# Third group's statistics and the factors on GpSimd's queue, and the first group's products with V without zero blocks

## The chip, the cores and the metric

The kernel runs on one core of a Trainium2 chip, as one program. A core has TensorE (PE in the profile; its weight loads are listed as PEld), VectorE (DVE), ScalarE (ACT), GpSimd (POOL) and SyncE (SP), which here only issues transfers. Each engine takes its own instructions strictly in the program's order and waits for the others by semaphores. Transfers are issued from SP, ACT or POOL, and 16 DMA engines carry them. The metric is the device time of one execution in microseconds (us); lower is better. The profile adds one recorded execution with the start, length and cause of waiting of each instruction.

## The reference, cut to what matters

Two layers work on x of 1024 tokens by 1024 features, all in float32. The first layer is dilated sliding-window attention with 18 heads of 64 features in three groups of six; the second is a latent attention that the change does not touch. In group 0 a query sees the 64 keys on either side of it, in group 1 the same at a stride of 4, in group 2 at a stride of 16. The three groups are merged with weights that come from the softmax statistics.

```
DIL_GROUPS = ((128, 1), (512, 4), (2048, 16))

s = einsum('bdhnqe,bdhnke->bdhnqk', qs, kb) * (Dh ** -0.5) + bias[:, None]
s = where(valid, s, NEG_INF)          # |key - query| <= R, R = window // (2 * dil) = 64
m = s.max(-1, keepdims=True)
p = exp(s - m)
denom = p.sum(-1, keepdims=True)
o = einsum('bdhnqk,bdhnke->bdhnqe', p, vb) / denom
lse = (m + log(denom))[..., 0]

# mixer_dilated
wts = softmax(stack(lses, axis=0), axis=0)
o = concatenate([outs[g] * wts[g][..., None] for g in range(len(DIL_GROUPS))], axis=2)
y = o.reshape(B, S, WIDTH_A) * silu(gate)
return y @ w_out
```

## The kernel before, in words

**Precision.** Most products are made of two or three matmuls on a reduced float32 type (`F32R`). An operand is split into a high part, which ScalarE rounds, and a low part, which VectorE or GpSimd gets by subtraction. A projection is then high by high, high by low and low by high (`mm3`, lines 89 to 91). A product with V in groups 0 and 1 splits only the probabilities (tiles `pt0h` and `pt0l`, line 550), since V's tile holds its own high and low halves side by side. Group 2 multiplies plain float32.

**Attention of layer A.** There are nine pairs of heads, three to a group. The attention of pair p is woven with the projection of pair p+1, a block of 128 weight columns at a time; `weave` picks at each step the generator that is furthest behind, by costs that the program states (`a_cost`). A pair has eight units of two query tiles (256 queries of one head). Each unit passes through `front` (scores on PE, line 487 and 488; bias and minimum on DVE, line 495; exponential on ACT, line 501), `middle` (transposes on PE, line 512; high part on ACT, line 528; low part on DVE, line 529) and `back` (product with V on PE, line 550).

**Products with V in group 0.** Two query tiles of 128 see three key tiles: the first only by the first query tile, the second by both, the third only by the second. `back` multiplies each of the three by 256 columns, so a unit has six matmuls of 256 columns (three key tiles, high and low part). The columns of the query tile that does not see a key tile are blocks of zeros in `pt0h` and `pt0l`, which are set once at the start (line 609). Two units share a PSUM bank, each with its own half.

**Merging.** After pair 8, `merge_lines` transposes the statistics (minimum and sum) of the groups. Those of groups 1 and 2 are in the order of the stride and are put in token order through DRAM: per group two writes (line 671) and twelve loads of 4 KB (line 675). VectorE then computes the factors, which go to DRAM (line 701) and come back as rows spread over 64 partitions (`factors`, line 709). `y_block` multiplies a pair's output by its factors (DVE, line 717) and by the gate (POOL, line 718).

**Gate blocks.** While this goes on, PE computes the gate projection: nine blocks of 128 columns, two of them during pair 8's attention and seven (blocks 2 to 8) in `layer_a_gate`. Each block needs 512 KB of weights, which SP loads (`w_load`, line 96, tile `wraw`), ACT rounds (line 101, `wh`) and POOL completes (line 102, `wl`). A block is 48 matmuls of 512 columns (the `pj` rows).

**What sets the order.** PE and SP run in the order in which the code is written. On the other engines a scheduler orders the instructions within its dependences. SP's order around the merge is: loads of group 1's and group 2's statistics, then the writes of the factors, then the weights of gate block 4 and the blocks after it. Line numbers are those of the profile of the kernel before.

Of the kernel before, what the change touches and what calls it, by code (L numbers as in the profile page):

```python
# [15 lines left out]
F32 = mybir.dt.float32  # L16
F32R = mybir.dt.float32r
# [6 lines left out]
P = 128  # L24
# [17 lines left out]
def f32(ap):  # L42
    return ap.bitcast(F32)


def weave(*gens):

    live = [[g, 0.0, float(total)] for g, total in gens]
    while live:
        it = min(live, key=lambda e: e[1] / e[2])  # L50
        try:
            it[1] += next(it[0])
        except StopIteration:
            live.remove(it)


def steps(gen, n):
    for _ in itertools.islice(gen, n):
        yield 1.0
# [7 lines left out]
class Trunk:  # L67
# [380 lines left out]
    def a_units(self, p):  # L448
        g = p // 3
        return 4 if g < 2 else 2  # L450

    def a_attn(self, p):

        nc = self.nc
        g, d = p // 3, self.a_dst[p]
        o = self.o[p] = self.gt(F32, "o")
        stat = self.stat[g]
        n = 8
        st = {}
        stage = self.zq[g == 2]  # L460

        def staged(i):

# [43 lines left out]
        def middle(i):  # L507
            sb = st.pop(i)
            pt = self.bank("t")
            nb = 4 if g < 2 else 2  # L510
            for j in range(nb):
                nc.tensor.transpose(pt[:, j * P : j * P + P], sb[:, j * P : j * P + P], self.ident)
            if g == 2:
                h = self.KP.tile([P, 256], F32, tag="ot", bufs=3, name=self.nm("pt2"))
                nc.vector.tensor_copy(h, pt[:, 0:256])
                st[i] = (h, None)
                return
            src = pt.rearrange("p (a b c) -> p a b c", a=2, b=2)
            if g == 0:
                h, l = self.pt0[i % 2]  # L520
                vh, vl = (
                    t.rearrange("p (a m) -> p a m", m=384)[:, :, :].rearrange("p a (b c) -> p a b c", c=P)[:, :, 0:3:2, :]
                    for t in (h, l)
                )
            else:
                h, l = self.pt0[i % 2]
                vh, vl = (t[:, 0:512].rearrange("p (b a c) -> p a b c", a=2, b=2) for t in (h, l))
            nc.scalar.copy(vh, src)
            nc.vector.tensor_tensor(vl, src, f32(vh), op=ALU.subtract)
            st[i] = (h, l)  # L530

        def back(i):
            e, up = i // 4, i % 4
            h, l = st.pop(i)
            if up % 2 == 0:
                st["o"] = self.bank("o")
            po = st["o"]
            if g == 2:
                for a in range(2):
                    t = 2 * up + a  # L540
                    c0 = (up % 2) * 256 + a * P
                    nc.tensor.matmul(
                        po[:, c0 : c0 + P], d["vt"][:, t, :], h[:, a * P : a * P + P], start=True, stop=True
                    )
            else:
                out = po[:, (up % 2) * 256 : (up % 2) * 256 + 256]
                nk = 3 if g == 0 else 2
                for k in range(nk):
                    for x, part in enumerate((h, l)):
                        nc.tensor.matmul(  # L550
                            out, d["vt"][:, 2 * up + k, e, :], part[:, k * 256 : k * 256 + 256],
                            start=(k == 0 and x == 0), stop=(k == nk - 1 and x == 1),
                        )
            if up % 2 == 1:
                z = up // 2
                mine, other = slice(64 * e, 64 * e + 64), slice(64 - 64 * e, 128 - 64 * e)
                ov = o[mine, :]
                if g == 0:
                    src, dst = (lambda x: x), ov[:, z * 512 : z * 512 + 512]
                elif g == 1:  # L560
                    src = lambda x: x.rearrange("p (r j) -> p r j", r=2)
                    dst = ov.rearrange("p (j r) -> p r j", r=4)[:, 2 * z : 2 * z + 2, :]
                else:
                    src = lambda x: x.rearrange("p (i j) -> p i j", i=4)
                    dst = ov.rearrange("p (j i) -> p i j", i=8)[:, 4 * z : 4 * z + 4, :]
# [25 lines left out]
                back(i - 2)  # L591
                yield cost[2]

    a_cost = ((480.0, 440.0, 720.0), (480.0, 440.0, 480.0), (480.0, 220.0, 480.0))

    def layer_a_attention(self):
        nc = self.nc
        self.o = {}
        for g in (1, 2):
            self.bias_line(g)  # L600
            self.bias_write(g)
        self.rows_d = self.DR.tile([2, 1, 1024], F32, name="rows_d")
        nc.vector.tensor_copy(self.ones_r, self.ones.to_broadcast([P, P]))
        self.pt0 = []
        for i in range(2):
            hl = []
            for x in "hl":
                t = self.KP.tile([P, 768], F32R, name=f"pt0{x}{i}")
                nc.gpsimd.memset(f32(t), 0.0)
                hl.append(t)  # L610
            self.pt0.append(hl)
        self.zq = []
        for x, dt in (("r", F32R), ("f", F32)):
            self.zq.append([[self.KP.tile([P, 256], dt, name=f"zq{x}{e}{i}") for i in range(2)] for e in range(2)])
            for e in range(2):
                for t in self.zq[-1][e]:
                    nc.gpsimd.memset(f32(t)[64 - 64 * e : 128 - 64 * e, :], 0.0)
# [31 lines left out]
    def merge_lines(self):  # L649


        nc = self.nc
        X, Y = self.ht(F32, "X"), self.ht(F32, "Y")
        part = lambda t, i, n=1: t[0:48, i * P : (i + n) * P]
        stat_d = self.DR.tile([2, 2, 48, P], F32, name="stat_d")
        self.f_d = self.DR.tile([3, 6, 1024], F32, name="f_d")
        for g in (1, 2, 0):
            pl = self.bank("pl")
            for s in range(2):
                nc.tensor.transpose(  # L660
                    pl[0:48, s * P : s * P + P], self.stat[g][:, s].rearrange("p h t -> p (h t)"), self.ident
                )
            if g == 0:
                for s in range(2):
                    nc.scalar.copy(part(X, 3 * s), pl[0:48, s * P : s * P + P])
                continue
            t = part(Y, 2 * g, 2)
            nc.scalar.copy(t, pl[0:48, 0:256])
            n = 32 if g == 1 else 16
            for s in range(2):  # L670
                nc.sync.dma_start(stat_d[g - 1, s], t[:, s * P : s * P + P])
            for s in range(2):
                ld = stat_d[g - 1, s]
                for h in range(6):
                    nc.sync.dma_start(
                        X[8 * h : 8 * h + 8, (3 * s + g) * P : (3 * s + g + 1) * P].rearrange("p (r j) -> p r j", j=n),
                        bass.AP(ld.tensor, ld.offset + 1024 * h, [[n, 8], [8 * n, P // n], [1, n]]),
                    )
# [19 lines left out]
        V.reciprocal(part(Y, 6), part(Y, 3))  # L698
        for g in range(3):
            V.tensor_tensor(part(Y, g), part(Y, g), part(Y, 6), op=ALU.mult)  # L700
            nc.sync.dma_start(self.f_d[g].rearrange("h (b t) -> (h b) t", t=P), part(Y, g))
        self.fs = {}

    def factors(self, b):
# [842 lines left out]
```

## Time and profile before

| | before |
|---|---|
| median of 3 runs | 1391.44 us |
| the three runs | 1387.54, 1391.44, 1395.55 us |
| the profiled execution: its time, its span | 1394.88 us, 1393.1 us |
| PE busy | 1346.1 us, 97% of the span |
| DVE, ACT, POOL busy | 918.1, 812.9, 570.5 us |
| mean granted clock of PE | 0.993 |
| attention of layer A | about 65 to 480 us of the span |
| merge and gate blocks 2 to 8 | 483 to 566 us |

The tables used are the page of the profile; the list of who waited for whom by engine; the timelines of single engines, where equal neighbours are merged and a row has start, length, engine, line, operation and, in brackets, the idle time before it and what ended it; the table of stretches, which has for each stretch its length, then busy time and number of instructions of PE, PEld, DVE, ACT and POOL, the clock that PE was granted, the share of the DMA engines and GB/s; and the answers for one line or tile, which give minimum, median and maximum length in ns. A matmul's row shows its whole passage through the array, 0.28 to 0.40 us, which overlaps with the next one's; what a matmul takes of PE's time is the distance between two starts.

### The profile page before, as it was taken

Reading aid. Unit: us, or ns where it says so; the run is one execution under the profiler, and the core shown is the slowest. Engines: PE = TensorE matmul, PEld = TensorE weight load, DVE = VectorE, ACT = ScalarE, POOL = GpSimd, SP = SyncE. Lnnn points to the kernel's source line nnn. Section 1 sums busy time; section 2 is a strip of 40 time slices with the busy share of each in tenths; the row PEclk is TensorE's granted clock in tenths of the full one; section 3 lists DMA queues with packets and bytes.
Section 4 is the critical chain, followed back from the end, with each engine's and each line's share of the span. In section 5 each row is a group of like instructions: output and inputs, shape, how many; then the busy total and the mean of one; then the engine's idle time right before and its main releaser. Section 6 shows DMA issues by size and latency. Waiting matters only on the chain.

```text
span 1393.1 us, 20960 instructions
## 1 busy us (share of the span) xinstructions
PE 1346.1 (97%) x7463; PEld 1153.6 (83%) x7463; DVE 918.1 (66%) x1688; ACT 812.9 (58%) x1599; POOL 570.5 (41%) x653
## 2 busy tenths in 40 slices
PE   6999999999999989999999999999999999999897
PEld 5788888888888878888987888888889888898786
DVE  7655454554455433646744178898988889888787
ACT  3565565565444432436742188788687878888321
POOL 6342243132123135803742254634453463444653
PEclk9999999999999999999999999999999999999999
DMA  9322211022244346544144001010011100014132
GB/s 362 95 70 36 61 45 55 24 61 65 83 152 130 100 114 154 191 143 158 47 130 155 22 22 29 16 30 16 22 30 24 30 16 16 16 61 130 53 109 88
DMA packets 42808, 110.05 MB, mean 79 GB/s; under 512 B 6853, under 2 KB 13205, under 8 KB 42704
## 3 DMA queue, kind: packets, MB, share of 16 engines
q1 hardware_dynamic: 38696, 96.60, 22.6%
q0 software_dynamic: 3552, 12.06, 3.5%
q8 instruction: 59, 0.97, 0.3%
q14 instruction: 45, 0.37, 0.1%
q10 hardware_dynamic: 456, 0.05, 0.0%
HBM read 92.22 MB, written 8.61 MB: 72 GB/s over the span
## 4 chain that ended last, share of the span: by engine, by line
PE 68%; DVE 16%; ACT 6%; issue 5%; DMA 3%; SPq 1%; POOL 0%; DVEq 0%; ACTq 0%; POOLq 0%
PE pj L91 7%; PE pj L89 7%; PE pj L90 6%; PE o L1305 5%; PE t L1282 5%; DVE mb L1263 3%; PE s L91 3%; PE s L89 3%; PE s L90 3%; PE po L91 3%; PE po L89 3%; PE po L90 3%; PE pg L89 2%; PE pg L91 2%; PE pg L90 2%
## 5 line engine op out<-in xcount | busy, mean ns | idle before, releaser
L89 PE MATMUL pj<-uh,wh 128*128 128x512 f32 x528 | 216.5, 410 | 2.1 <-ACT wh L101 2.1
L91 PE MATMUL pj<-uh,wl 128*128 128x512 f32 x528 | 207.9, 394 | 1.6 <-POOL wl L102 1.6
L90 PE MATMUL pj<-ul,wh 128*128 128x512 f32 x528 | 207.7, 393 | 0.0
L1286 DVE TENSOR_TENSOR ptl<-t,pth 128x512 fp32r<-128x512 f32 x256 | 165.3, 681 | 3.0 <-ACT pth L1285 0.9
L1263 DVE TENSOR_REDUCE mb<-s 128x1 f32<-128x1024 f32 x128 | 155.7, 1217 | 7.9 <-PE s L91 6.3
L1269 ACT ACTIVATE pr<-s,mb 128x1024 f32<-128x1024 f32 x128 | 143.4, 1120 | 29.2 <-DVE mb L1263 21.1
L1285 ACT CAST pth<-t 128x512 fp32r<-128x512 f32 x256 | 138.9, 590 | 36.2 <-PE t L1282 34.1
L102 POOL TENSOR_TENSOR wl<-wraw,wh 128x1024 fp32r<-128x1024 f32 x43 | 107.5, 2506 | 106.0 <-ACT wh L101 60.9
L1282 PEld LDWEIGHTS t<-ident,pr 128*128 128x128 f32 x1024 | 119.3, 140 | 19.7 <-DVE ptl L1286 2.6
L1282 PE MATMUL t<-ident,pr 128*128 128x128 f32 x1024 | 133.2, 272 | 1.9 <-DVE ptl L1286 1.9
L1305 PE MATMUL o<-pth,vq 128*128 128x256 f32 x512 | 130.4, 293 | 0.0
L1305 PE MATMUL o<-ptl,vq 128*128 128x256 f32 x512 | 125.5, 283 | 0.8 <-DVE ptl L1286 0.8
L501 ACT ACTIVATE sb<-sb,stat 128x256 f32<-128x256 f32 (+1 forms) x144 | 67.0, 467 | 97.5 <-DVE stat L495 97.3
L91 PEld LDWEIGHTS pj<-uh,wl 128*128 128x128 f32 x528 | 99.7, 189 | 24.3 <-POOL wl L102 2.1
L89 PEld LDWEIGHTS pj<-uh,wh 128*128 128x128 f32 x528 | 100.3, 190 | 16.8 <-ACT wh L101 2.5
L1288 POOL COPY den<-mb 128x64 f32<-128x64 f32 x128 | 30.1, 237 | 202.9 <-DVE mb L1287 193.3
L90 PEld LDWEIGHTS pj<-ul,wh 128*128 128x128 f32 x528 | 100.4, 190 | 14.3
L89 PE MATMUL s<-kb,q 128*128 128x512 f32 x256 | 104.4, 408 | 0.2 <-ACT pr L1269 0.2
L91 PE MATMUL s<-kb,q 128*128 128x512 f32 x256 | 101.3, 396 | 0.0
L90 PE MATMUL s<-kb,q 128*128 128x512 f32 x256 | 100.8, 394 | 0.0
L1305 PEld LDWEIGHTS o<-ptl,vq 128*128 128x128 f32 x512 | 97.8, 191 | 1.4 <-DVE ptl L1286 1.4
L1305 PEld LDWEIGHTS o<-pth,vq 128*128 128x128 f32 x512 | 97.7, 191 | 0.2
(281 smaller groups left out, 3262.6 us busy)
## 6 DMA issues: line engine op xcount, KB each, us to landing
wraw<-wa SPq DMA_DIRECT2D x36, 512.0 KB
ada<-ada_row SPq DMA_DIRECT2D x64, 256.0 KB
wraw<-wo_a SPq DMA_DIRECT2D x18, 512.0 KB
ada<-ada_ss SPq DMA_DIRECT2D x16, 512.0 KB
kb<-kb POOLq DMA_DIRECT2D x30, 256.0 KB, 3.0
f<-f_d SPq DMA_DIRECT2D x18, 256.0 KB
xc<-xt SPq DMA_DIRECT2D x8, 512.0 KB
xr<-x SPq DMA_DIRECT2D x8, 512.0 KB
```

The costliest lines, as they stand in the source:

```text
L89: mm(out, wh, xh, start=start, stop=False)
L90: mm(out, wh, xl, start=False, stop=False)
L91: mm(out, wl, xh, start=False, stop=stop)
L102: (lo_engine or self.nc.gpsimd).tensor_tensor(l[:, :width], raw[:, :width], f32(h[:, :width]), op=ALU.subtract)
L501: nc.scalar.activation(sb[:, a * w : a * w + w], sb[:, a * w : a * w + w], AF.Exp, bias=stat[:, 0, hh, t : t + 1], scale=-1.0, accum_out=s ...
L1263: nc.vector.tensor_reduce(m[:, 0:1], s, axis=AX.X, op=ALU.max, negate=True)
L1269: nc.scalar.activation(pr, s, AF.Exp, bias=m[:, 0:1], accum_out=m[:, 1:2])
L1282: nc.tensor.transpose(pt[:, c * P : c * P + P], pr[:, kt * P : kt * P + P], self.ident)
L1285: nc.scalar.copy(h, src)
L1286: nc.vector.tensor_tensor(l, src, f32(h), op=ALU.subtract)
L1288: nc.gpsimd.tensor_copy(st["den"][:, 64 * a : 64 * a + 64], m[:, 2:3].to_broadcast([P, 64]))
L1305: nc.tensor.matmul(po[:, 0:256], v, pts[j][x][:, c * 256 : c * 256 + 256], start=n == 0, stop=n == 15)
```

## The change

It has two parts.

**The queue.** Group 2's statistics (two writes, twelve loads) and all three factor writes are issued from POOL's queue; group 1's statistics stay on SP.

**Products with V in group 0.** The tiles `pt0h` and `pt0l` become 1024 wide and hold two units (four query tiles) without zeros. Four query tiles see five key tiles. An even unit multiplies key tile 1 (256 columns) and 0 (128 columns), an odd unit key tiles 3 and 2 (256 columns each) and 4 (128 columns), each for the high and the low part. So a pair of units has ten matmuls, six of 256 and four of 128 columns, in place of twelve of 256. All of them add into one bank; only the first sets the start flag. The stated cost of `back` in group 0 goes from 720 to 580.

To make room, the tiles with padded queries (`zq`) exist once: they are made for group 0 as `F32R` and again for group 2 as `F32`, where they are cleared again. The clearing of `pt0` falls away.

```
@@ def zero_padded, a_attn @@
+    def zero_padded(self, dt):
+        z = [
+            [self.KP.tile([P, 256], dt, tag=f"zq{e}{i}", bufs=1, name=self.nm("zq" + "fr"[dt == F32R])) for i in range(2)]
+            for e in range(2)
+        ]
+        for e in range(2):
+            for t in z[e]:
+                self.nc.gpsimd.memset(f32(t)[64 - 64 * e : 128 - 64 * e, :], 0.0)
+        return z
...
-        stage = self.zq[g == 2]
+        if p % 3 == 0 and g != 1:
+            self.zq = self.zero_padded(F32R if g == 0 else F32)
+        stage = self.zq
@@ middle @@
-            src = pt.rearrange("p (a b c) -> p a b c", a=2, b=2)
+            half = self.pt0[i // 2 % 2]
+            h, l = (t[:, i % 2 * 512 : i % 2 * 512 + 512] for t in half)
             if g == 0:
-                h, l = self.pt0[i % 2]
-                vh, vl = (
-                    t.rearrange("p (a m) -> p a m", m=384)[:, :, :].rearrange("p a (b c) -> p a b c", c=P)[:, :, 0:3:2, :]
-                    for t in (h, l)
-                )
+                vh, vl, src = h, l, pt
+                st[i] = half
             else:
-                h, l = self.pt0[i % 2]
-                vh, vl = (t[:, 0:512].rearrange("p (b a c) -> p a b c", a=2, b=2) for t in (h, l))
+                vh, vl = (t.rearrange("p (b a c) -> p a b c", a=2, b=2) for t in (h, l))
+                src = pt.rearrange("p (a b c) -> p a b c", a=2, b=2)
+                st[i] = (h, l)
             nc.scalar.copy(vh, src)
             nc.vector.tensor_tensor(vl, src, f32(vh), op=ALU.subtract)
-            st[i] = (h, l)
@@ back @@
+            elif g == 0:
+                z = up - up % 2
+                for k in ((1, 0), (3, 2, 4))[up % 2]:
+                    c0, c1 = max(256 * k - P, 0), min(256 * k + P, 1024)
+                    q0 = max(P * (k - 1), 0)
+                    for x, part in enumerate((h, l)):
+                        nc.tensor.matmul(
+                            po[:, q0 : q0 + (c1 - c0)], d["vt"][:, 2 * z + k, e, :], part[:, c0:c1],
+                            start=(k == 1 and x == 0), stop=(k == 4 and x == 1), skip_group_check=True,
+                        )
             else:
                 out = po[:, (up % 2) * 256 : (up % 2) * 256 + 256]
-                nk = 3 if g == 0 else 2
-                for k in range(nk):
+                for k in range(2):
...
-    a_cost = ((480.0, 440.0, 720.0), (480.0, 440.0, 480.0), (480.0, 220.0, 480.0))
+    a_cost = ((480.0, 440.0, 580.0), (480.0, 440.0, 480.0), (480.0, 220.0, 480.0))
@@ layer_a_attention @@
         for i in range(2):
-            hl = []
-            for x in "hl":
-                t = self.KP.tile([P, 768], F32R, name=f"pt0{x}{i}")
-                nc.gpsimd.memset(f32(t), 0.0)
-                hl.append(t)
-            self.pt0.append(hl)
-        self.zq = []
...
+            self.pt0.append([self.KP.tile([P, 1024], F32R, name=f"pt0{x}{i}") for x in "hl"])
@@ merge_lines @@
-            n = 32 if g == 1 else 16
+            n, queue = (32, nc.sync) if g == 1 else (16, nc.gpsimd)
             for s in range(2):
-                nc.sync.dma_start(stat_d[g - 1, s], t[:, s * P : s * P + P])
+                queue.dma_start(stat_d[g - 1, s], t[:, s * P : s * P + P])
...
-                    nc.sync.dma_start(
+                    queue.dma_start(
...
-            nc.sync.dma_start(self.f_d[g].rearrange("h (b t) -> (h b) t", t=P), part(Y, g))
+            nc.gpsimd.dma_start(self.f_d[g].rearrange("h (b t) -> (h b) t", t=P), part(Y, g))
```

**SP's queue at the merge.** `stat_d` and `X` are the statistics on their way through DRAM, `f_d` the factors, `wraw` the weights of gate blocks 3, 4, 5 and 6 in this order. First before, then changed:

```order
L96 DMA wraw_625_4150<-wa 128x1024
L671 DMA stat_d_4193<-Y_629_4192 48x128 x2
L675 DMA X_628_4191<-stat_d_4193 8x4x32 x12
L671 DMA stat_d_4193<-Y_629_4192 48x128 x2
L675 DMA X_628_4191<-stat_d_4193 8x8x16 x12
L701 DMA f_d_4194<-Y_629_4192 48x128 x3
L96 DMA wraw_638_4300<-wa 128x1024
L96 DMA wraw_644_4359<-wa 128x1024
L709 DMA f_645_4374<-f_d_4194 64x1024 x2
L709 DMA f_646_4377<-f_d_4194 64x1024 x2
L96 DMA wraw_652_4424<-wa 128x1024
```

```order
L96 DMA wraw_633_4122<-wa 128x1024
L682 DMA stat_d_4165<-Y_637_4164 48x128 x2
L686 DMA X_636_4163<-stat_d_4165 8x4x32 x12
L96 DMA wraw_646_4272<-wa 128x1024
L96 DMA wraw_652_4331<-wa 128x1024
L720 DMA f_653_4346<-f_d_4166 64x1024 x2
L720 DMA f_654_4349<-f_d_4166 64x1024 x2
L96 DMA wraw_660_4396<-wa 128x1024
```

The weights of gate blocks 4 and 5 (`wraw_638` and `wraw_644`, now `wraw_646` and `wraw_652`) stand behind seventeen transfers fewer.

**POOL's queue at the merge.** `wl` are the low parts of the weights of gate blocks 3, 4, 5 and, in the last row, 6; `o` are the outputs multiplied by the gate. First before, then changed:

```order
L102 TENSOR_TENSOR wl_636_4283<-wraw_625_4150,wh_635_4282 128x1024
L102 TENSOR_TENSOR wl_642_4342<-wraw_638_4300,wh_641_4341 128x1024
L102 TENSOR_TENSOR wl_650_4407<-wraw_644_4359,wh_649_4406 128x1024
L718 TENSOR_TENSOR o_99_616<-o_99_616,graw_576_3877 128x1024
L718 TENSOR_TENSOR o_151_1021<-o_151_1021,graw_607_4049 128x1024
L102 TENSOR_TENSOR wl_657_4471<-wraw_652_4424,wh_656_4470 128x1024
```

```order
L102 TENSOR_TENSOR wl_644_4255<-wraw_633_4122,wh_643_4254 128x1024
L682 DMA stat_d_4165<-Y_637_4164 48x128 x2
L686 DMA X_636_4163<-stat_d_4165 8x8x16 x12
L102 TENSOR_TENSOR wl_650_4314<-wraw_646_4272,wh_649_4313 128x1024
L712 DMA f_d_4166<-Y_637_4164 48x128 x3
L102 TENSOR_TENSOR wl_658_4379<-wraw_652_4331,wh_657_4378 128x1024
L729 TENSOR_TENSOR o_99_596<-o_99_596,graw_584_3849 128x1024
L729 TENSOR_TENSOR o_155_1001<-o_155_1001,graw_615_4021 128x1024
L102 TENSOR_TENSOR wl_665_4443<-wraw_660_4396,wh_664_4442 128x1024
```

Fourteen transfers now stand ahead of gate block 4's low part, and three more ahead of block 5's.

**PE at the first odd unit of group 0.** `t` are transposes, `o` the product with V. First before, then changed:

```order
L512 MATMUL t_770<-ident,sb_705 128x128 x4
L550 MATMUL o_740<-pt0h_563,vt_663 128x256
L550 MATMUL o_740<-pt0l_565,vt_663 128x256
L550 MATMUL o_740<-pt0h_563,vt_663 128x256
L550 MATMUL o_740<-pt0l_565,vt_663 128x256
L550 MATMUL o_740<-pt0h_563,vt_663 128x256
L550 MATMUL o_740<-pt0l_565,vt_663 128x256
```

```order
L564 MATMUL o_728<-pt0h_559,vt_651 128x256
L564 MATMUL o_728<-pt0l_560,vt_651 128x256
L564 MATMUL o_728<-pt0h_559,vt_651 128x256
L564 MATMUL o_728<-pt0l_560,vt_651 128x256
L564 MATMUL o_728<-pt0h_559,vt_651 128x128
L564 MATMUL o_728<-pt0l_560,vt_651 128x128
```

The odd unit still has six matmuls, two of them 128 wide; the even unit has four, of which two are 128 wide.

More of the change, by code (lines that the diff above doesn't have):

```diff
@@ L551, in back @@
                             out, d["vt"][:, 2 * up + k, e, :], part[:, k * 256 : k * 256 + 256],
-                            start=(k == 0 and x == 0), stop=(k == nk - 1 and x == 1),
+                            start=(k == 0 and x == 0), stop=(k == 1 and x == 1),
                         )
@@ L605, in layer_a_attention @@
         for i in range(2):
-            hl = []
-            for x in "hl":
-                t = self.KP.tile([P, 768], F32R, name=f"pt0{x}{i}")
-                nc.gpsimd.memset(f32(t), 0.0)
-                hl.append(t)
-            self.pt0.append(hl)
-        self.zq = []
[L613 to L617, printed above, removed]
+            self.pt0.append([self.KP.tile([P, 1024], F32R, name=f"pt0{x}{i}") for x in "hl"])
         for p in range(NPAIR_A):
```

## The prediction

> **What bounds the kernel now.** I read the busy shares first.
>
> ```profile
> PE 1346.1 (97%) x7463; PEld 1153.6 (83%) x7463; DVE 918.1 (66%) x1688; ACT 812.9 (58%) x1599; POOL 570.5 (41%) x653
> ```
>
> PE is busy nearly throughout, so the time changes in two ways: PE gets less work, or PE stands still for less time. The list of waits tells what it stands still for. Of its rows, three lie in the stages that the change touches:
>
> ```profile
> PE o L550 <- DVE pt0l L529: 5.5, 6, 1.1
> PE pj L89 <- ACT wh L101: 2.1, 1, 2.1
> PE pj L91 <- POOL wl L102: 1.6, 1, 1.6
> ```
>
> The last two are one place, the start of gate block 4. PE's timeline and the table of stretches show it:
>
> ```profile
> 504.87 0.39 PE L91 MATMUL pj<-uh,wl 128*128 128x512 f32 x1
> 507.32 0.50 PE L89 MATMUL pj<-uh,wh 128*128 128x512 f32 x1 [2.07 <-ACT wh L101]
> 507.66 0.46 PE L90 MATMUL pj<-ul,wh 128*128 128x512 f32 x1
> 509.76 0.80 PE L91 MATMUL pj<-uh,wl 128*128 128x512 f32 x1 [1.64 <-POOL wl L102]
> 510.35 0.63 PE L89 MATMUL pj<-uh,wh 128*128 128x512 f32 x1
> ...
> 507.50:510.00 2.50, 0.86 (x3) 0.36 (x4) 0.00 (x0) 1.31 (x2) 2.28 (x2) 0.57 1.01 210
> 512.00:514.00 2.00, 2.00 (x6) 1.57 (x5) 1.77 (x2) 0.00 (x0) 0.84 (x2) 0.50 1.06 256
> 516.00:518.00 2.00, 2.00 (x10) 1.65 (x9) 0.99 (x2) 1.49 (x2) 1.01 (x1) 1.00 0.14 31
> ```
>
> PE waits twice for block 4's weights, and afterwards its granted clock (the third number from the end) is 0.57, then 0.50, and 1.00 again from about 516. The price is read from ACT, which takes each half block from PSUM:
>
> ```profile
> 488.97 0.60 ACT L804 ACTIVATE gate<-pj 128x512 f32<-128x512 f32 x1 [3.61 <-PE pj L91]
> 494.41 0.60 ACT L804 ACTIVATE gate<-pj 128x512 f32<-128x512 f32 x1 [4.84 <-PE pj L91]
> 517.37 0.60 ACT L804 ACTIVATE gate<-pj 128x512 f32<-128x512 f32 x1 [0.47 <-PE pj L91]
> ```
>
> A half block takes 494.41 - 488.97 = 5.44 us. From 494.41 to 517.37 lie three of them, which took 22.96 us in place of 16.32: the stall costs **6.6 us**, 3.7 of them standing still and about 2.9 slow clock and restart.
>
> Why the weights are late is in SP's timeline:
>
> ```profile
> 483.55 0.79 SPq L671 DMA_DIRECT2D stat_d<-Y  x2
> 484.98 4.06 SPq L675 DMA_DIRECT2D X<-stat_d  x12
> 489.13 1.61 SPq L671 DMA_DIRECT2D stat_d<-Y  x2
> 491.51 4.12 SPq L675 DMA_DIRECT2D X<-stat_d  x12
> 501.03 1.24 SPq L701 DMA_DIRECT2D f_d<-Y  x3
> 502.33 0.89 SPq L96 DMA_DIRECT2D wraw<-wa  x2
> 503.31 2.42 SPq L709 DMA_DIRECT2D f<-f_d  x4
> ...
> 506.21 1.06 ACT L101 ACTIVATE wh<-wraw 128x1024 fp32r<-128x1024 f32 x1 [4.37 <-DMA wraw<-wa]
> ```
>
> From 495.6 SP waits for the factors that VectorE is still computing; block 4's weights, queued behind, go out at 502.33 and are there at 506.21. PE needed them at 505.1.
>
> **The queue.** Group 1's loads leave SP at 484.98 + 4.06 = 489.0, and the next entry is now block 4's weights: issued at 489.1, 13.2 us earlier, there at about 493 by the 3.9 us above. ACT rounds them between the two gate halves, ahead of the exponential that waits for the statistics. POOL completes them behind its fourteen new transfers. Their price is bounded by POOL's own transfers and its gap:
>
> ```profile
> L940 POOL DMA_DIRECT2D xn_d<-z x8: 533/576/762, 630.2 to 676.4; - x8
> L1155 POOL DMA_DIRECT2D kb<-kb x30: 519/542/577, 720.9 to 1199.9; - x30
> DMA to landing us min/median/max: 2.9/3.0/6.8
> 481.91 2.37 POOL L102 TENSOR_TENSOR wl<-wraw,wh 128x1024 fp32r<-128x1024 f32 x1 [15.30 <-PE pj L90]
> 507.35 2.36 POOL L102 TENSOR_TENSOR wl<-wraw,wh 128x1024 fp32r<-128x1024 f32 x1 [23.06 <-ACT wh L101]
> ```
>
> I take 0.55 us of POOL for each and 3.0 us to landing (the landing row is L1155's). The two writes go out at 484.3 to 485.4 and land at 488.4; twelve loads end at 495.0; block 4's low part runs from 495.0 to 497.4, and PE needs it at 505.5: 8 us to spare. POOL's gap of 23 us is the cover for all of it. Uncovered, the stall would return by what exceeds those 8 us. So the stall of 6.6 us goes.
>
> Late next are the factors. Group 2's statistics now land at 498.0. Before, VectorE had them at 494.87, and wrote the last factors 6.5 us later:
>
> ```profile
> 494.87 0.37 DVE L690 TENSOR_TENSOR Y<-Y,X 48x128 f32<-48x128 f32 x1 [6.15 <-DMA X<-stat_d]
> 500.69 0.69 DVE L700 TENSOR_TENSOR Y<-Y 48x128 f32<-48x128 f32 x3
> 510.99 2.38 DVE L717 TENSOR_TENSOR o<-o,f 128x1024 f32<-128x1024 f32 x1 [9.61 <-DMA f<-f_d]
> 557.60 1.48 DVE L833 TENSOR_TENSOR yt<-o,yt 128x512 fp32r<-128x512 f32 x1 [14.29 <-ACT yt L832]
> ```
>
> So they are ready at 504.5, on DRAM at 508.0 (0.55 + 3.0), and SP, which waits for that, issues the factor loads at 508 in place of 503.31: 4.7 us later, and behind them block 6's weights. Block 5's low part follows the three writes on POOL at 506.1 to 508.5; PE needs it at 516. Block 6's weights go out at about 510.5 and POOL, after two outputs, is through with them at about 521; PE needs them at 527, 6 us to spare. The last multiplication by factors ended 14.3 us before VectorE's next work; 6.6 earlier for PE and 4.7 later for the factors leave 3.0. This part is worth **-6.6 us**, at least 0 if another stall takes its place, without gain beyond 6.6.
>
> **Products with V.** Rows of a unit before, of the projection after it, and of group 2's plain float32 product:
>
> ```profile
> 189.81 0.28 PE L550 MATMUL o<-pt0h,vt 128*128 128x256 f32 x1
> 190.53 0.40 PE L89 MATMUL pj<-uh,wh 128*128 128x512 f32 x1
> 190.76 0.40 PE L90 MATMUL pj<-ul,wh 128*128 128x512 f32 x1
> ...
> 470.82 0.61 PE L542 MATMUL o<-pt,vt 128*128 128x128 f32 x4
> L542 PE MATMUL o<-pt,vt x96: 270/275/377, 367.5 to 479.0; 128*128 128x128 f32 x96
> ```
>
> Six matmuls of 256 columns take 190.53 - 189.81 = 0.72 us, 0.12 each; one of 512 takes 0.23. No row shows an `F32R` matmul of 128 columns. Three prices:
> - By columns: 256 more cost 0.11, so 128 fewer save 0.055: 0.065 us.
> - By the rows of 128 columns that there are: four in 0.61, the last of them 0.275 long, so (0.61 - 0.275) / 3 = 0.11 us between starts.
> - As plain float32: the code has 3 pairs x 8 units x 2 = 48 such products and the trace 96 records, so one product is two records, 0.22 us.
>
> Two units cost 12 x 0.12 = 1.44 us before, 6 x 0.12 = 0.72 plus four narrow ones after: 0.98, 1.16 or 1.60. Over twelve pairs of units that is -5.5, **-3.4** or +1.9 us. I take 0.11: every matmul here loads its own weights, and 0.11 is what rows of this width show.
>
> [...] No run here shows a narrow `F32R` matmul yet.
>
> Nothing else in that stage gets longer. The casts and subtractions keep 512 columns, each unit waits only for its own, and transposes and products keep nearly their distance in PE's order. So the 5.5 us of waits for `pt0l` stay, to within 2 either way. The clearings are hidden:
>
> ```profile
> 0.95 0.73 POOL L609 MEMSET pt0h<- 128x768 f32 x1
> 4.96 1.17 POOL L617 MEMSET zqf<- 64x256 f32 x4
> 372.54 0.74 POOL L468 COPY zqf<-q 64x256 f32<-64x256 f32 x2 [11.74 <-ACT q L371]
> ```
>
> The ones at the start ended at 6.1 us, before PE's first work, so dropping them gains nothing; the four for group 2 (1.2 us) fall where POOL idles 11.7 us, and would cost those 1.2 without it.
>
> **The sum.** -6.6 - 3.4 = -10.0: span 1393.1 to 1383.1, the profiled execution 1394.9 to 1384.9. It is 3.4 us above the median of the runs, so the median would go from 1391.4 to 1381.4; I say **1382**, because the runs are spread over 8 us and some of them may have lost less in the stall.
>
> **The rivals.**
> - *The narrow matmuls cost as plain float32.* For it: group 2's rows, and that the kernel filled up to 256 columns with zeros. Against: those rows are two records each, and an `F32R` product has one. +1.9 - 6.6 = -4.7: 1387.
> - *The clock does not fall in every run.* For it: the runs differ by 8 us; two short waits set it off. Then the queue brings only the 3.7 us of waiting: -7.1, 1384. [...]
> - *The stall moves to block 6*, whose weights now wait behind the later factors. For it: 4.7 us later. Against: 6 us to spare. If landing takes 6.8 us as in the slowest transfer, twice in the chain, it returns: about -3.4 in all, 1388.
> - *Narrow matmuls by columns*: -12.1, 1379.
> - *Slower: POOL's queue becomes the chain.* Group 2's loads are cut into runs of 64 bytes, those of L1155 and L940 are rows of 4 KB. At d us for each, block 4's low part ends at 484.3 + 2d + 3.0 + 12d + 2.4 = 489.7 + 14d, and PE needs it at 505.5: a stall from d = 1.13. At d = 2 it is 12.2 us; block 5's low part, behind the factors (3.0 + 6.5 after the loads) and three writes, ends at 499.2 + 17d against a need at 516.4 plus the first stall, which adds 3d - 1.4 = 4.6; with 2.9 for the clock each time it is 22.6, and with -6.6 - 3.4 in all +12.6: 1404. Against: all 38 transfers in the rows took 0.52 to 0.76.
>
> **How the numbers follow.** Chances: forecast 0.52, plain float32 0.22, clock 0.10, block 6 0.06, by columns 0.05, POOL 0.05. Medians of a few runs of this kernel tell 0.5%, 7 us, from no change. Below 1384.5 counts as faster: 0.85 of the forecast (0.44), 0.15 of plain float32 (0.03), half of the clock case (0.05), by columns (0.05), in all 0.58 with rounding. Slower is the POOL case and a little for the spread, 0.06; the rest, 0.36, is the same. The range 1376 to 1390 holds all cases but the last, with the spread of the runs.
>
> **What would show it.** In the profile after: the weights of block 4 issued about 13 us before the factor loads; no wait of PE at the `pj` rows and a clock of 1.00 between block 3 and block 5; POOL's transfers near 0.55 us; the distance between starts of 128-wide matmuls near 0.11. The queue part is wrong if any `pj` row waits over 1 us; the product part if that distance is over 0.18 or under 0.08.

## The result and the profile after

| | before | after |
|---|---|---|
| median | 1391.97 us (7 runs) | 1383.70 us (7 runs, 1381.56 to 1387.39) |
| ratio, with its 95% interval | | 0.9945 (0.9931 to 0.9959), that is -7.7 us (-9.6 to -5.7) |
| the profiled execution: its time, its span | 1394.88, 1393.1 us | 1385.48, 1383.7 us |

The change made the kernel faster by 0.55%. The page of the profile after and its list of waits follow, with the rows that answer to those shown of before. Here and below a fence holds selected rows of a view, and rows between them are left out.

```profile
PE 1340.7 (97%) x7439; PEld 1148.6 (83%) x7439; DVE 916.6 (66%) x1688; ACT 813.4 (59%) x1599; POOL 578.2 (42%) x666
```

```profile
PE o L572 <- DVE pt0l L541: 3.8, 4, 1.1
PE t L525 <- ACT sb L514: 3.2, 3, 1.3
PE o L564 <- DVE pt0l L541: 1.2, 1, 1.2
```

PE executes 24 matmuls fewer, no `pj` row waits any more, and the waits for `pt0l` are 5.0 us in place of 5.5. Line 525 is the transposition (line 512 before), line 541 the subtraction (529), lines 564 and 572 the products with V in group 0 and 1 (550).

The timelines of SP, POOL, ACT and PE around gate block 4 (start, length, engine, line, operation; in brackets the idle time before it):

```profile
482.29 4.08 SPq L686 DMA_DIRECT2D X<-stat_d  x12
486.41 5.67 SPq L96 DMA_DIRECT2D wraw<-wa  x2
499.53 2.43 SPq L720 DMA_DIRECT2D f<-f_d  x4
502.64 0.33 SPq L96 DMA_DIRECT2D wraw<-wa  x1
```

```profile
481.54 1.23 POOL L682 DMA_DIRECT2D stat_d<-Y  x2
483.70 6.70 POOL L686 DMA_DIRECT2D X<-stat_d  x12 [0.93 <-DMA stat_d<-Y]
491.61 2.54 POOL L102 TENSOR_TENSOR wl<-wraw,wh 128x1024 fp32r<-128x1024 f32 x1 [1.21 <-DVE Y L703]
497.81 1.58 POOL L712 DMA_DIRECT2D f_d<-Y  x3 [3.66 <-ACT graw L809]
```

```profile
490.36 1.06 ACT L101 ACTIVATE wh<-wraw 128x1024 fp32r<-128x1024 f32 x1 [3.47 <-DMA wraw<-wa]
502.61 0.60 ACT L815 ACTIVATE gate<-pj 128x512 f32<-128x512 f32 x1 [3.69 <-PE pj L91]
518.93 0.60 ACT L815 ACTIVATE gate<-pj 128x512 f32<-128x512 f32 x1 [0.49 <-PE pj L91]
502.86 0.39 PE L91 MATMUL pj<-uh,wl 128*128 128x512 f32 x1
```

The first weights behind group 1's loads go out at 486.41, 13.1 us ahead of the factor loads. ACT has rounded block 4's at 491.4, and POOL has completed them at 494.15, 8.7 us before PE needs them (502.86, PE's first row with `wl` of this block). From the end of block 3 (ACT's copy at 502.61) three half blocks, block 4's two and the first of block 5, take 518.93 - 502.61 = 16.32 us, the 5.44 us each that the profile before had without a stall. Before, the three that ended with block 4's first half took 22.96.

To see where the time went I cut every profile at the same five places: PE's first `pj` row, the 12th and the 24th copy of `ot` on ACT (the last units of groups 0 and 1), PE's transposition of the statistics, and PE's first `po` row. From there to the end the two do not differ (826.9 us in both).

| stage, us | before | after | |
|---|---|---|---|
| up to the first projection | 70.59 | 68.71 | -1.9 |
| group 0 | 142.06 | 139.29 | -2.8 |
| group 1 | 141.33 | 140.68 | -0.6 |
| group 2 | 128.67 | 131.29 | **+2.6** |
| merge and gate | 83.48 | 76.84 | **-6.6** |

The sum with the end is -9.4, the difference of the spans. The first row is no part of the change: it lay between 67.2 and 70.7 us in the fourteen profiles, whatever the kernel. The +2.6 in group 2 was not forecast. It arises for the most part in pair 8's last unit (PE's rows, the first of before and two of after, and the table of stretches after, with length, busy time and instructions of PE, PEld, DVE, ACT and POOL, the clock, the share of the DMA engines and GB/s):

```profile
476.25 0.71 PE L512 MATMUL t<-ident,sb 128*128 128x128 f32 x2 [0.94 <-ACT sb L501]
470.00 0.71 PE L553 MATMUL o<-pt,vt 128*128 128x128 f32 x4 [0.33 <-DVE pt L528]
472.00 0.78 PE L525 MATMUL t<-ident,sb 128*128 128x128 f32 x2 [1.28 <-ACT sb L514]
```

```profile
472.00:474.00 2.00, 1.94 (x6) 1.48 (x7) 0.42 (x1) 1.95 (x4) 0.00 (x0) 0.63 0.00 0
474.00:476.00 2.00, 2.00 (x9) 1.72 (x8) 0.00 (x0) 0.52 (x1) 0.00 (x0) 0.52 0.00 0
```

PE waits twice, 1.6 us in all, and then runs 4 us at a mean clock of 0.63 and 0.52, which costs another 1.7 us. Before, it waited 0.94 us there and kept a clock of 1.00. DVE's timeline after tells why the exponential is late:

```profile
468.07 0.75 DVE L750 SCALAR_TENSOR_TENSOR ada<-ada,sc 128x512 f32<-128x512 f32 x1 [1.68 <-DMA ada<-ada_row]
470.45 0.75 DVE L750 SCALAR_TENSOR_TENSOR ada<-ada,sc,ada 128x512 f32<-128x512 f32 x1 [0.51 <-DMA ada<-ada_row]
471.12 0.28 DVE L508 CUSTOM_DVE_ANT_0 sb<-s,bias 128x128 f32<-128x128 f32 x1
```

The last unit's bias and minimum (line 508) are queued behind two steps of the second layer's modulation that wait for a row from DRAM.

### The profile page after: what moved, and what is told of

It is laid out like the page before. It is cut to its first block, busy times and chain, and to the rows that moved or that the text cites. A ratio compares the mean times of both kernels' runs of the same rounds, so it can differ in the third digit from the quotient of the medians.

```text
span 1383.7 us, 20921 instructions
## 1 busy us (share of the span) xinstructions
PE 1340.7 (97%) x7439; PEld 1148.6 (83%) x7439; DVE 916.6 (66%) x1688; ACT 813.4 (59%) x1599; POOL 578.2 (42%) x666
## 4 chain that ended last, share of the span: by engine, by line
PE 70%; DVE 15%; ACT 6%; issue 5%; DMA 3%; SPq 0%; DVEq 0%; ACTq 0%
PE pj L89 7%; PE pj L91 7%; PE pj L90 7%; PE o L1316 5%; PE t L1293 5%; DVE mb L1274 3%; PE s L91 3%; PE s L89 3%; PE s L90 3%; PE po L91 3%; PE po L89 3%; PE po L90 3%; PE pg L89 2%; PE pg L91 2%; PE pg L90 2%
```

## The experiments

Ratios are to the kernel before on the same chip, with 95% intervals; "us" is the ratio times that kernel's median there (1391.4 in the first group of runs, 1392.4 in the second, 1391.6 and 1391.7 in the last two).

### The parts apart

**The queue alone** (the kernel before with the change's hunks in `merge_lines`).

> The kernel before with the queue part alone: group 2's statistics and the three factor writes on POOL's queue, products with V as before. Theory: the stall at gate block 4 goes and nothing takes its place; three half blocks at that place take 16.3 us again in place of 22.96, so the median falls by 6.6 us from about 1392, to 1385. Rival 'the clock does not fall in every run': the median falls by the waits alone, 3.7 us, to 1388. Rival 'POOL's queue becomes the chain': a pj row waits over 1 us for wl, and the time is 1392 or more. In the profile the theory wants no wait of PE at a pj row of block 4, and a clock of 1.00 from block 3 to block 5.

Measured: 0.9962 (0.9949 to 0.9975), **-5.3 us** (-7.1 to -3.5). No `pj` row waits, and the clock from 500 to 512 is 1.00. Merge and gate take 76.84 us, to the hundredth what they take in the change.

**The products alone** (the change with the hunks in `merge_lines` undone).

> The kernel before with the product part alone: ten matmuls for two units, no zero blocks; statistics and factors on SP as before. Theory: -3.4 us, to 1388.5, and the stall at block 4 stands as before (waits of about 2.1 and 1.6 us there). Rival by columns: -5.5, 1386.5. Rival by the starts that the profile of the change shows (the four narrow matmuls 0.06 and 0.11 us apart, the 512-wide one behind them 0.055 longer): 12 x 0.18 = -2.2, 1389.7. The profile of the change also shows pair 8 ending with two waits of 1.28 and 0.33 us and a clock of 0.52 behind them (about 2.7 us against before). If that belongs to the new products, it is in this profile and not in that of the queue part alone; if it comes from late loads of ada_row, it may be in either or in neither.

Measured: 0.9983 (0.9975 to 0.9991), **-2.4 us** (-3.5 to -1.3). By columns (-5.5) is out. The forecast's -3.4 and the expectation's -2.2 both lie in the interval, so the time alone does not tell them apart. Group 0 takes 139.27 us, again -2.8, and group 2 takes 130.5. The stall at block 4 is there, but look at PE's rows and the stretches:

```profile
501.49 0.50 PE L89 MATMUL pj<-uh,wh 128*128 128x512 f32 x1 [0.84 <-ACT wh L101]
503.92 0.50 PE L91 MATMUL pj<-uh,wl 128*128 128x512 f32 x1 [1.70 <-POOL wl L102]
```

```profile
502.00:504.00 2.00, 0.30 (x2) 0.08 (x1) 0.00 (x0) 0.87 (x1) 2.00 (x2) 1.00 1.06 244
504.00:506.00 2.00, 2.00 (x9) 1.66 (x10) 1.21 (x1) 0.00 (x0) 2.00 (x1) 1.00 0.96 213
```

PE waits 2.5 us and the clock stays at 1.00. Merge and gate take 79.95 us, 3.1 over 76.84, where the stall of the profile before cost 6.6.

### Which transfers had to leave SP

Only line 701 on POOL (the first two lines of the diff, e3), and in the next run only lines 671 and 675 for group 2 (the last two, e4):

```
-            nc.sync.dma_start(self.f_d[g]...)
+            nc.gpsimd.dma_start(self.f_d[g]...)
...
-            n = 32 if g == 1 else 16
+            n, queue = (32, nc.sync) if g == 1 else (16, nc.gpsimd)
```

> The kernel before with one half of the queue part: only the three factor writes go to POOL's queue, group 2's statistics stay on SP. Theory (what holds the weights is SP waiting for the factors): SP is through with the loads at 495.6, sends block 4's weights then, they land at 499.5, ACT rounds them by 501 and POOL completes them by 505 at the latest, when PE needs them at 505.1 to 505.5: no stall, -6.6 us, 1385, as with both halves. Rival (the fourteen transfers of group 2 must leave SP as well): the weights are late by 1 to 2 us, a wait stays at block 4, and the gain is 0 to -3.

> The kernel before with the other half: group 2's statistics on POOL's queue, the factor writes still on SP. Theory: SP still stands before the factor writes, with block 4's weights behind them. In the profile of the change the loads on POOL landed as early as SP's did before, so the factors are ready at the same time and the stall is the same: 0 us, 1392. By my forecast's landing of 3.0 us, factors 3.8 us later, the stall grows by 3.8 us: 1395.5. Rival (shorter queue on SP alone frees the weights): -6.6, 1385.

Measured: the factors alone 0.9962 (0.9950 to 0.9973), -5.3 us, as much as both halves; the statistics alone 1.0005 (0.9996 to 1.0013), +0.7 us (-0.6 to +1.8). SP's timeline, first of the factors alone, then of the statistics alone:

```profile
487.87 4.12 SPq L675 DMA_DIRECT2D X<-stat_d  x12
492.03 0.83 SPq L96 DMA_DIRECT2D wraw<-wa  x2
```

```profile
496.44 1.25 SPq L701 DMA_DIRECT2D f_d<-Y  x3
497.74 0.89 SPq L96 DMA_DIRECT2D wraw<-wa  x2
```

With the factor writes gone, the weights leave right behind group 2's loads. With the writes in place they stand behind them, and the stall stays: waits of 1.63 and 1.70 us, 82.36 us for merge and gate. So what held the weights was SP waiting for the factors. Moving the statistics was hardly needed, but it bought the margin: with the factors alone block 4's low part is complete 0.28 us too late (the one wait left; merge and gate take 77.42 us, 0.6 over 76.84), with both 8.7 us early.

### The two parts together, once more

> The changed kernel once more, beside the next three on one chip. Theory (the two parts add): -7.7 us from before, as before and after gave and as the two parts gave apart (-5.3 and -2.4). The question to its profile: pair 8 ended in the first profile with waits of PE of 1.28 and 0.33 us and then 4 us at a clock of about 0.5. If that belongs to the change, it is here again; if it is DVE's accumulation standing before late loads of ada_row and a clock that falls in some executions only, waits of 0.9 to 2.6 us in all are here, and the clock may stay at 1.00.

Measured: 0.9945 (0.9932 to 0.9959), the same again; -5.3 and -2.4 add up to it. The end of pair 8 is slow here too, with one wait of 2.00 us at the last transposition:

```profile
472.00:474.00 2.00, 1.50 (x5) 1.12 (x6) 0.84 (x4) 1.95 (x6) 0.00 (x0) 0.75 0.00 0
474.00:476.00 2.00, 2.00 (x8) 1.61 (x7) 0.00 (x0) 0.97 (x1) 0.00 (x0) 0.50 0.00 0
```

### The price of a narrow matmul

```
-                        nc.tensor.matmul(
+                        for r in range(4 if k in (0, 4) else 1):
+                            nc.tensor.matmul(
...
```

> The changed kernel with each 128-wide F32R matmul of group 0 issued four times in place of once, 144 more of them; the sums are then not the reference's. By the forecast (0.11 us each): +15.8 us against the changed kernel, distances between the starts of equal ones 0.11. By columns (0.065): +9.4, distances 0.065. As plain float32 (0.22): +31.7.

Measured: 1.0038 (1.0026 to 1.0050), that is +12.0 us against the changed kernel by the medians (1397.13 and 1385.15). Group 0 takes 154.80 us in place of 139.28: 15.5 us for 144 matmuls, **0.108 us each**. The profile had no slow stretch in pair 8 this time, which may be part of why the whole grew by less; the 12.0 of the whole lies between the forecast's 15.8 and the 9.4 by columns, and it is the stage that decides. PE's timeline of an odd unit:

```profile
191.41 0.56 PE L565 MATMUL o<-pt0h,vt 128*128 128x128 f32 x4
191.80 0.61 PE L565 MATMUL o<-pt0l,vt 128*128 128x128 f32 x4
192.25 0.45 PE L89 MATMUL pj<-uh,wh 128*128 128x512 f32 x1
```

Four take 0.39 and 0.45 us; the 0.39 holds one short first distance of 0.06, of which more below, and the 0.45 is 0.112 each. The forecast's 0.11 holds, plain float32 (0.22) and columns (0.065) fall.

In the changed kernel itself a narrow one looks cheaper than it is (PE's timeline of the change, an odd unit):

```profile
191.23 0.28 PE L564 MATMUL o<-pt0h,vt 128*128 128x256 f32 x1
...
191.71 0.22 PE L564 MATMUL o<-pt0h,vt 128*128 128x128 f32 x1
191.77 0.28 PE L564 MATMUL o<-pt0l,vt 128*128 128x128 f32 x1
191.88 0.45 PE L89 MATMUL pj<-uh,wh 128*128 128x512 f32 x1
192.17 0.39 PE L90 MATMUL pj<-ul,wh 128*128 128x512 f32 x1
```

The starts are 0.06 and 0.11 apart, but the 512-wide one behind them keeps PE 0.29 us in place of 0.23. From the first product to line 90 it is 192.17 - 191.23 = 0.94 us; before, six matmuls of 256 and the same projection took 190.76 - 189.81 = 0.95. So halving the columns of two matmuls saved next to nothing. What group 0 gained, 2.8 us, is what the 24 matmuls that are gone had cost: 0.116 each, about the 0.12 of one of 256.

### From where POOL's queue decides

Two more loads ahead of each of group 2's twelve:

```
+                    for r in range(1, 3 if g == 2 else 1):
+                        queue.dma_start(X[64 + 8 * h : 72 + 8 * h, (3 * s + r) * P : ...], ...)
```

> The changed kernel with 24 more loads among group 2's twelve on POOL's queue, into rows that nobody reads: as if a load took three times as long, the rival of my forecast in which POOL's queue becomes the chain. By the trace of the change a load takes 0.56 us of POOL and block 4's low part is complete 8.7 us before PE needs it. 24 x 0.56 = 13.4 us, less the 1.2 that POOL stood still there: complete at 506.4, needed at 502.9, a wait of 3.5 us at pj <- POOL wl. Time against the changed kernel: +3.5 if the clock stays, +6.4 if it falls as in the profile before. If POOL's issue is not what PE comes to wait for (another engine late first, or loads that overlap), no such wait and 0 to +2.

Measured: 0.9989 (0.9978 to 1.0000), which is +5.7 us against the change by the medians and between the two numbers expected. POOL's timeline, PE's one wait at the gate, and the stretches:

```profile
501.10 2.36 POOL L102 TENSOR_TENSOR wl<-wraw,wh 128x1024 fp32r<-128x1024 f32 x1
```

```profile
503.51 0.50 PE L91 MATMUL pj<-uh,wl 128*128 128x512 f32 x1 [3.06 <-POOL wl L102]
```

```profile
504.00:506.00 2.00, 2.00 (x8) 1.56 (x7) 1.90 (x5) 2.00 (x3) 0.00 (x0) 0.70 0.00 0
506.00:508.00 2.00, 2.00 (x6) 1.59 (x5) 0.62 (x3) 0.74 (x1) 1.12 (x1) 0.50 0.00 0
```

POOL completes block 4's low part at 503.46, PE takes it at 503.51. Merge and gate take 81.82 us, 5.0 over 76.84. The rival's mechanism is real and its place was right; only the price of a load (0.56 us, where 1.13 would have been needed) kept it away.

### What the change loses in group 2

Group 2 took 128.7 to 129.1 us in the four profiles with the products of before, and 129.6 to 131.9 in the five with the new ones and an unchanged pair 8. First, the tiles of padded queries alone, made anew for group 2, with the old products and the queue part:

> The kernel before with the queue part and, of the product part, only the padded queries' tiles made anew for group 2 (one set for both types, cleared again); products with V with their zero blocks. It asks where the change loses in group 2: from the last unit of group 1 to the transposition of the statistics the four profiles with the products of before took 128.7 to 129.1 us, the five with the new ones and their tiles 129.6 to 131.9. If the tiles made anew are the cause, this profile has over 129.5, and the time is 1 to 2 us above the queue part alone (1386.1). If it is not the tiles, 128.5 to 129.2, and the time of the queue part alone.

Measured: 128.98 us for group 2, and 0.9961 (0.9949 to 0.9973), the time of the queue part alone. The tiles are not the cause. Then pair 8's end, by one step of cost in `a_attn` that makes `weave` put six projection matmuls ahead of the last transposition, and in the second of the two runs (e12, `i in (1, n)` in place of `i == n`) ahead of the first one too:

```
+            if p == NPAIR_A - 1 and i == n:
+                yield 700.0
             if 0 <= i - 1 < n:
                 middle(i - 1)
```

> The changed kernel with one more step of cost ahead of pair 8's last transposition, so that six more pj matmuls (1.37 us) stand between the last scores and it on PE. Theory: the wait there falls from 1.28 us to between 0 and 0.4, and with it what the clock sometimes takes behind it: -1.0 to -3.0 us against the changed kernel. Rival (what PE does not wait for there it waits for later, since the statistics come last in any case): 0.

> The changed kernel with the step of cost at both ends of pair 8 (ahead of its first and of its last transposition), and products with V two steps behind the scores as in the change, since three steps were slower. Theory: both waits of pair 8 for the exponential go (0.9 to 1.75 us at its start, 1.3 to 2.1 at its end), group 2 takes 128.5 us as in e10, and the ratio to before is that of the change less about 3 us: 0.9925, some 1381. Rival (the run on the end alone, 0.9928, was luck of its runs; what is gained is within the spread): 0.9945, 1384.

Measured: 0.9928 (0.9912 to 0.9944) and 0.9934 (0.9919 to 0.9949), medians 1381.73 and 1382.93 us. By the medians e6 is 3.4 us below the changed kernel on its chip, a little more than the 1.0 to 3.0 expected. Group 2 takes 129.07 and 127.62 us (0.45 us of work has moved behind the stage in the second); the wait at the end of pair 8 is gone in the first and 0.34 us in the second, and neither has a slow stretch there. The intervals overlap with the change's 0.9945. Taken together, the twelve runs of these two have a mean of 1382.4 us and the twelve of the change 1384.3 (standard errors 0.5 each, not all on the same chip): 1.9 us less. In the profiles group 2 is shorter by 2.2 us or more, and 1.7 of that is the slow stretch. The second edit gained nothing that can be told: the wait at pair 8's start, which was to go, is still 0.96 us. e6 has the lowest ratio of this case, -10.0 us (-12.3 to -7.8) from before, though e12 cannot be told from it.

### Taking the waits for `pt0l` away as well

```
-        for i in range(n + 2):
+        lag = 3 if g < 2 else 2
+        for i in range(n + lag):
...
-            if 0 <= i - 2 < n:
-                back(i - 2)
+            if 0 <= i - lag < n:
+                back(i - lag)
```

> The kernel of the run on pair 8's tail (e6) with one edit more: in groups 0 and 1 a unit's product with V is issued one step later, three steps behind its scores instead of two. The profile of the change has five waits of PE for pt0l, 0.7 to 1.2 us each, 5.0 in all. Theory: with a step between the subtraction and the product they go: -3.5 to -5.0 us against e6, to about 1377 to 1378. Rival (DVE and ACT set the pace in that stage, and PE waits as long at the next scores or for a PSUM bank): 0, 1381.7.

> The same as e9 with one more step of cost also ahead of pair 8's first transposition, where all profiles show PE waiting 0.9 to 1.75 us for the exponential. Theory: that wait falls below 0.4, another -0.9 to -1.5 us against e9. Rival: the step is missing later in pair 8, where PE then waits as long: 0.

Measured: 0.9975 (0.9962 to 0.9987) and 0.9962 (0.9949 to 0.9974): the first is about **6 us slower** than e6, the same kernel without the lag. My theory fell, and the rival was too mild. All waits for `pt0l` are gone, and the first row of the waits is now (the change had 3.2 us there):

```profile
PE t L525 <- ACT sb L514: 8.7, 7, 2.5
```

The table of stretches shows what stands behind the two longest waits of e9. It is cut every 3.41 us, the length of the slow stretch that starts at 250.24:

```profile
246.83:250.24 3.41, 1.37 (x7) 1.05 (x8) 2.24 (x6) 1.55 (x5) 0.00 (x0) 1.00 0.10 21
250.24:253.65 3.41, 3.41 (x11) 2.83 (x10) 0.82 (x2) 1.76 (x3) 0.00 (x0) 0.50 0.65 166
294.62:298.03 3.41, 2.20 (x12) 1.54 (x10) 2.88 (x3) 1.62 (x3) 1.32 (x2) 1.00 0.00 0
298.03:301.45 3.42, 2.11 (x11) 1.61 (x11) 2.10 (x7) 1.68 (x5) 0.00 (x0) 1.00 0.21 37
301.45:304.86 3.41, 3.41 (x20) 2.98 (x19) 1.19 (x2) 1.66 (x2) 0.00 (x0) 1.00 0.66 193
```

PE comes to the next transposition earlier, the exponential does not, and two of the short waits have become waits of 2.5 us (2.48 us up to 248.8 and 2.47 up to 299.3), the first of them with a slow clock behind it and the second without. Group 0 gains 0.8 us, group 1 takes 144.7 instead of 140.5. In e10 group 2 takes 128.5 us, for 130.7 in e9; but 1.7 us of that is a slow stretch that e10 does not have there, 0.45 is work that has moved behind the stage, and the wait at pair 8's start, which was to fall below 0.4, is still 1.44 us. Group 1 takes 146.3 us there, with two slow stretches.

## Why the prediction was right, point by point

The time came out at 1383.7 and 1385.2 us for a forecast of 1382, inside the range 1376 to 1390; the first is below the 1384.5 that the forecast takes as the bound of faster, the side it called likeliest, the second above it. The two terms were -6.6 and -3.4; the parts alone gave -5.3 and -2.4. Both mechanisms were right and both sizes about 1 us too large. The forecast of 1382 cannot be told by the time from the 1384 of the rival on the clock.

- **The stall goes, and nothing takes its place: right.** The weights were issued 13.1 us ahead of the factor loads (about 13 forecast), the low part was complete 8.7 us early (8 forecast), POOL's loads took 0.56 us (0.55 taken), no `pj` row waits, and the clock stays at 1.00. The experiments add which half did it: the factor writes.
- **Its price of 6.6 us: too high.** The step that failed is reading it from one execution. Four profiles have the stall: with 3.7 us of waiting it cost 6.6 us of merge and gate, with 3.3 it cost 5.5 (statistics alone), with 3.1 it cost 5.0 (the added loads), with 2.5 it cost 3.1 and the clock did not move (products alone). The clock makes the difference: the profile of before ran 6.8 us at half clock behind the stall, a loss of 3.4 us, the next two 3.4 us, a loss of 1.7, and the last none. So the rival "the clock does not fall in every run" was right in that (1.00 behind the 2.5 us of products alone), but its price, the waits alone, is too low: the three kernels without the stall and with the old products (e1, e11, and e3 with its 0.28 us of wait) have a mean of 1385.8 us over 17 runs and the kernel before 1391.5 over the 72 beside the experiments, -5.7. Their mean granted clocks are 0.9959 and 0.9936, a difference worth about 3 us of 1390 by my estimate, which suggests that most runs of before did pay for the clock.
- **Late next are the factors, by 4.7 us: wrong, and it did no harm.** Two sizes in that chain were wrong. It let VectorE begin when the last of the twelve loads has landed. Line 701, the first step that uses group 2's statistics, takes the minimum and needs only the first six (a row of DVE's timeline after, then the landing times of POOL's loads and of the factor writes):

```profile
490.58 0.38 DVE L701 TENSOR_TENSOR Y<-Y,X 48x128 f32<-48x128 f32 x1 [4.68 <-DMA X<-stat_d]
DMA to landing us min/median/max: 1.8/2.1/3.9
DMA to landing us min/median/max: 1.7/1.7/1.7
```

  The last of the twelve was issued at 489.8 and none lands in under 1.8 us, so VectorE did not wait for it. And it took a landing of 3.0 us from the transfers of line 1155; the factor writes landed after 1.7. The factor loads left SP at 499.53, which on the clock of the profile before (2.68 us later at this place) is 502.2, 1.1 us *earlier* than the 503.31 there. Block 6 was never near a stall: POOL completed its low part at 515.3, and by 5.44 us for a half block PE needs it at about 524.6.
- **The narrow matmul at 0.11 us: right** (0.108). The term came out at 2.8 us in group 0 for 3.4, because two narrow ones also hold up the matmul behind them by 0.06; in place, a narrow one costs about as much as one of 256. "Wrong if under 0.08" was a poor test: single distances in the change are 0.06, and only the sum of three tells the price.
- **"Nothing else in that stage gets longer": right for group 0, wrong behind it.** Group 2 is longer in all five profiles with the new products, by 0.5 to 3.2 us, and of that some 1.7 us are the clock in two of them (4 us at 0.57, and 4 at 0.63, in the rows above). Over the runs, the twelve of the change have a mean clock of 0.9949 against 0.9959 for the 17 with the old products and no stall. It happens where DVE stands before `ada_row` at the end of pair 8. In this stage PE, DVE, ACT, POOL and SP have the same instructions in the same order with the old products and the new. What grew is DVE's waiting for `ada_row`: 13.2 to 14.3 us over the stage in the five profiles with the old products, 15.3 to 17.1 in these five. Why the rows come later with the new products is not settled; it is not the tiles of padded queries.
- **The clearings are hidden: right.** With the tiles made anew and the old products (e11), no stage is longer.
- **The rivals.** Plain float32 and columns were excluded by the repeated matmuls, the move to block 6 by the profile, POOL's queue by the price of its loads; the added loads then produced its mechanism.

## What to carry to other kernels

A queue that issues in order should not hold a wait for computed data ahead of loads that depend on nothing: moving three writes was worth 5 us, and the fourteen transfers moved beside them only bought margin. Price a stall from several executions, since a wait may or may not have a slow clock behind it: here 3.7 us of waiting cost 6.6 with a clock of 0.50 behind them, and 2.5 us cost 3.1 at a clock of 1.00. Count matmuls and not columns where they cost what they do here, 0.108 us for 128 columns and 0.12 for 256, each with its own weights; and before moving PE's work away from one short wait, ask which engine's pace the wait shows, because PE may meet it at the next step with a longer one, as in the two waits of 2.5 us with the later product.

## What the hardware showed beside that

- **The clock does not follow the length of the wait alone.** It fell to 0.50 behind waits of 0.33 and 1.28 us (the change), 2.0 (the same again), 3.06 (added loads), 1.63 and 1.70 (statistics alone). It stayed at 1.00 behind 0.84 and 1.70 us within 3.3 us (products alone), and behind a wait of 2.12 us at the end of pair 8 (repeated matmuls). It was 0.50 for 6.83 us before (507.85 to 514.68), and for 3.41 us after (472.51 to 475.92) and with the later product (250.24 to 253.65). The next slow stretch starts 808.96 us behind the first of these, 237 times 3.413, and 904.53 us behind the second, 265 times. In the 3.41 us ahead of each of the three PE stands still for 2.07, 1.67 and 2.04 us, and for 1.64 in the first half of the 6.83. The two like waits with the later product differ in one execution (rows above): 2.04 us of the first fall into one row, and the next row runs at 0.50; the second is divided, 1.21 and 1.31 us of standing still, and the clock stays at 1.00. What decides whether it falls is not settled by these runs.
- **An `F32R` matmul of 128 columns costs 0.108 us in these runs, one of 256 costs 0.12, one of 512 0.23**, each with its own weights.
- **Small transfers on POOL's queue** took 0.50 to 0.61 us of POOL for loads of 4 KB and the factor writes, with 1.7 to 2.1 us to landing in the median. On SP group 1's loads, of the same 4 KB, take 0.30 us of its queue:

```profile
L686 SPq DMA_DIRECT2D X<-stat_d x12: 281/300/312, 482.3 to 486.1; - x12
L686 POOL DMA_DIRECT2D X<-stat_d x12: 561/561/607, 483.7 to 489.8; - x12
```
